# A NaN-skipping row maximum: ten write-backs that go through their elements in another order

## The chip, the cores and the metric

The kernel runs on one core of one Trainium2 chip. The metric is the device time of one execution in microseconds (us). Three engines work on the data: VectorE (DVE in the profile), ScalarE (ACT) and GpSimd (POOL). SyncE (SP) only issues the transfers.

## The reference

```python
def setup_inputs():
    batch, seq, dim = 32, 2048, 2048
    x = np.random.randn(batch, seq, dim).astype(np.float32)
    mask = np.random.rand(batch, seq, dim) < 0.1
    x[mask] = np.nan
    return {"x": x, "axis": -1}

def reference(x, axis):
    return np.nanmax(x, axis=axis).astype(np.float32)
```

The input is 65,536 rows of 2,048 float32 values (537 MB), a tenth of them NaN. The output is the largest value of each row that is no NaN.

## The kernel before, in words

**Cleaning.** [...] Only the upper 16 bits of each float are touched: `xt[:, a:b].bitcast(i16)[:, 1::2]`, a view of int16 elements that lie 4 bytes apart. Two steps do it. ScalarE makes a *key* (line 384 calls the helper whose record is L222): it reads the upper halves of xt and writes a packed uint16 tensor, kt, in which a NaN has become a number of its own. Then the *write-back* turns the key into the upper half again and writes it to xt in place; a NaN comes out as minus infinity. Most write-backs are GpSimd's (line 405, record L232), some are ScalarE's (in `release`, line 357, record L222 again, with `xt<-kt` instead of `kt<-xt`). VectorE then takes the maximum of the cleaned part (line 430, record L239).

**Tiles.** The work is a hand-written list, `TILES`. Sizes are in units of Q = 512 elements per partition, and a full tile is 28 of these (14,336 elements in each of 128 partitions, 7.3 MB). Each entry gives the loads, the pieces that are cleaned, and the pieces of the maximum. A usual tile is `([28], [7, 9, 12], [16, 12])`: one load, three keys with three GpSimd write-backs of 3584, 4608 and 6144 elements, and two reductions. A negative piece is ScalarE's to write back. Entries 8, 16, 24, 32 and 40 of the list (counted from 0) are

```python
([28], [9, 12, -7], [8, 20])
```

There GpSimd writes back 4608 and 6144 elements, ScalarE the last 3584. The first reduction (8) needs only the piece of 9; the second (20) needs the piece of 12 and ScalarE's piece.

**Order of the work.** Three buffers hold tiles (`xts`), three hold keys (`kts`, 6144 elements each). Every engine goes through its instructions in the order of the program and waits on semaphores, which the class `Order` puts down. A load waits for the last reduction of the tile that had its buffer three tiles earlier. A key waits for its load and for the write-backs of what was in its key buffer. In the entries above the order on ScalarE is: key of 9, key of 12, key of 7, write-back of 7, and then the key of 7 of the next tile. The key of 7 in the tile waits for GpSimd's write-back of the piece of 9, since it takes that piece's key buffer.

Of the kernel before, what the change touches and what calls it, by code (L numbers as in the profile page):

```python
# [10 lines left out]
Q = D // 4  # L11
# [51 lines left out]
LEAD = 128  # L63

LANES = 14

# [104 lines left out]
def kernel(  # L173
# [18 lines left out]
    i16, u16 = mybir.dt.int16, mybir.dt.uint16  # L192
# [22 lines left out]
    with tc.tile_critical():  # L215
# [75 lines left out]
        number = 0  # L291
# [6 lines left out]
        for gi, (s, g) in enumerate(zip(rows, GROUPS)):  # L298
            xg = xr[r0 : r0 + P * s].rearrange("(p s) d -> p (s d)", p=P)
            og = of[r0 : r0 + P * s].rearrange("(p s) -> p s", p=P)  # L300
            r0 += P * s
            first = sum(rows[:gi])
            acc = accs[:, first : first + s]
            base = 0
            for loads, pieces, reds in g:
                assert sum(loads) == total(pieces) == sum(reds)
                xt, before = xts[number % BUFS], free[number % BUFS]
                number += 1
                landed = []
                at = 0  # L310
                for c in loads:
                    c *= Q
                    e = order.add(
                        "sp",
                        nc.sync,
                        lambda: nc.sync.dma_start(  # L316
                            out=xt[:, at : at + c], in_=xg[:, base + at : base + at + c]
                        ),
                        before + lanes[turn],
                        lane=f"load{turn}",  # L320
                        step=16,
                    )
                    lanes[turn] = [e]
                    turn = (turn + 1) % LANES
                    landed.append((at, at + c, e))
                    at += c
                clean = []
                after = []
                at = done = 0
                reds = [n * Q for n in reds]  # L330
                part = []
                held = []
                pairs = {}
                if number not in APART:
                    pairs = joints(pieces, [n // Q for n in reds])
                flat = sum((p if isinstance(p, tuple) else (p,) for p in pieces), ())
                half = {}
                piece = 0

                def cleaned(a, b, k, i, e):  # L340

                    nonlocal clock
                    clock += 1
                    both = [(a, b, k, flat[i] < 0, clock)]
                    if i in pairs:
                        if pairs[i] not in half:
                            half[pairs[i]] = both
                            return
                        both += half.pop(pairs[i])
                    for a, b, k, back, when in both:  # L350
                        kfree[k].append((back, when, e))
                        clean.append((a, b, e))

                def name(i):
                    return f"pair{number}_{pairs[i][0]}" if i in pairs else None

                def release():
                    for a, b, k, kp, e, i in held:
                        e = act(
                            [e],  # L360
                            name(i),
                            out=xt[:, a:b].bitcast(i16)[:, 1::2],
                            in_=kp,
                            func=ACT.Copy,
                            bias=float(TOP),
                            scale=-1.0,
                        )
                        cleaned(a, b, k, i, e)
                    held.clear()

                for parts in pieces:
                    parts = parts if isinstance(parts, tuple) else (parts,)
                    c = int(sum(map(abs, parts))) * Q
                    here = [l for a, b, l in landed if a < at + c and b > at]
                    kold = []
                    if used + c > KEYS:
                        key = (key + 1) % NKEYS
                        used = 0
                        kold, kfree[key] = last(kfree[key]), []
                        assert all(k != key for q in half.values() for _, _, k, _, _ in q)  # L380
                        if at + c == sum(loads) * Q:

                            kold = kold + last(kfree[(key + 1) % NKEYS])
                    e_key = act(
                        here + kold,
                        out=kts[key][:, used : used + c],
                        in_=xt[:, at : at + c].bitcast(i16)[:, 1::2],
                        func=ACT.Prelu,
                        bias=EDGE,
                        scale=-1.0,  # L390
                        alpha=float(TOP - LOW) / (EDGE - NAN),
                    )
                    release()
                    for c in parts:
                        back, wait, c = c < 0, isinstance(c, float), int(abs(c)) * Q
                        kp = kts[key][:, used : used + c]
                        used += c
                        to = xt[:, at : at + c].bitcast(i16)[:, 1::2]
                        at += c
                        if back:  # L400
                            held.append((at - c, at, key, kp, e_key, piece))
                            if not wait or at == sum(loads) * Q:
                                release()
                        else:
                            e = pool(
                                [e_key],
                                name(piece),
                                out=to,
                                in0=kp,
                                scalar1=-1.0,  # L410
                                scalar2=float(TOP),
                                op0=ALU.mult,
                                op1=ALU.add,
                            )
                            cleaned(at - c, at, key, piece, e)
                        piece += 1
                        open_ = [h[0] for h in held] + [p[0] for q in half.values() for p in q]
                        while reds and done + reds[0] <= min([at] + open_):
                            n = reds.pop(0)


                            lo = done - 1 if done % D else done
                            done += n
                            row = (base + lo) // D
                            if done % D:
                                m, to = 1, xt[:, done - 1 : done].bitcast(f32)
                            else:
                                m = max(n // D, 1)
                                to = acc[:, row : row + m]
                            e = dve(  # L430
                                [e for a, b, e in clean if b > lo and a < done] + part,
                                nc.vector.tensor_reduce,
                                out=to,
                                in_=xt[:, lo:done]
                                .bitcast(f32)
                                .rearrange("p (c d) -> p c d", c=m),
                                axis=mybir.AxisListType.X,
                                op=ALU.max,
                            )
                            part = [e] if done % D else []  # L440
                            after.append(e)
                free[(number - 1) % BUFS] = after[-1:]
                base += at
            stores.append((og, acc.bitcast(i32)))
            if gi == LATE:
                late_after = after
            elif gi not in FLAGGED:
                continue
            lo, flagged = flagged, first + s
            if gi == LATE:  # L450
                late_acc = accs[:, lo:flagged]
            else:
                e = find(after, accs[:, lo:flagged])
                ready += [e] * (gi + 1 - len(ready))
            if gi == len(GROUPS) - 1:
                ready[LATE] = find_late(late_after, late_acc, late)
# [47 lines left out]
```

## Time and profile before

| | |
|---|---|
| median of 3 runs | 1252.51 us (1252.46 to 1252.6) |
| the profiled execution's own time | 1252.48 us |
| its span in the trace | 1250.7 us |
| busy: POOL / DVE / ACT | 1168.5 (93%) / 1111.4 (89%) / 965.6 (77%) us |
| HBM read | 536.87 MB, 429 GB/s over the span |

The span runs from the first to the last instruction; 1.8 us of the execution lie outside it. Busy time is the time in which an engine executes. A wait is idle time before an instruction, put down to what ended last before it.

### The profile page before, as it was taken

The numbers are of one execution on the slowest core, as the hardware profiler recorded it, in microseconds if no ns is written. First come the engines' busy times: TensorE is split into PE (matmuls) and PEld (weight loads), VectorE is DVE, ScalarE is ACT, GpSimd is POOL, SyncE is SP. The second block draws the span as 40 slices with busy tenths as digits, with TensorE's granted clock in tenths as the row PEclk, the third lists the DMA queues.
The fourth block names the chain that finished last, engine by engine and source line by source line (L and its number), as shares of the span: only waits on it lengthen the run. The fifth ranks groups of instructions, "written<-read, shape, count | busy, mean of one in ns | idle before, by whom it ended". The sixth has DMA issues, their size and how long they took to land.

```text
span 1250.7 us, 891 instructions
## 1 busy us (share of the span) xinstructions
DVE 1111.4 (89%) x179; ACT 965.6 (77%) x273; POOL 1168.5 (93%) x242
## 2 busy tenths in 40 slices
DVE  0888989888889888898988888998888899999999
ACT  3777887778777877788777877777777778999997
POOL 2999989998999899998999899999999999989998
DMA  9999999999999999999999999999999999999997
GB/s 415 440 418 433 440 440 438 413 440 440 440 433 418 440 440 438 429 424 440 440 436 424 431 440 438 436 424 433 440 438 435 422 436 436 425 434 429 431 428 301
DMA packets 15991, 537.20 MB, mean 430 GB/s; under 512 B 2544, under 2 KB 2544, under 8 KB 3568
## 3 DMA queue, kind: packets, MB, share of 16 engines
q1 hardware_dynamic: 15984, 537.14, 99.4%
q14 instruction: 7, 0.06, 0.0%
HBM read 536.87 MB, written 0.26 MB: 429 GB/s over the span
## 4 chain that ended last, share of the span: by engine, by line
DMA 40%; DVE 29%; POOL 22%; ACT 9%; issue 1%; SPq 0%
DMA xt<-in_x_dram 40%; DVE acc L239 29%; POOL xt L232 22%; ACT kt L222 8%; ACT xt L222 1%; SPq L316 0%; DVE acc L245 0%; SPq L499 0%; SPq L215 0%
## 5 line engine op out<-in xcount | busy, mean ns | idle before, releaser
L232 POOL TENSOR_SCALAR xt<-kt 128x3584 int16<-128x3584 uint16 (+11 forms) x236 | 1167.4, 4947 | 77.6 <-ACT kt L222 63.9
L239 DVE TENSOR_REDUCE acc<-xt 128x3 f32<-128x6144 f32 (+4 forms) x175 | 1107.5, 6379 | 135.6 <-POOL xt L232 128.1
L222 ACT ACTIVATE kt<-xt 128x3584 uint16<-128x3584 int16 (+9 forms) x247 | 913.4, 3734 | 278.0 <-DMA xt<-in_x_dram 257.9
L222 ACT ACTIVATE xt<-kt 128x512 int16<-128x512 uint16 (+6 forms) x24 | 52.8, 2202 | 0.7
L245 DVE SCALAR_TENSOR_TENSOR acc<-acc 128x414 f32<-128x414 f32 (+1 forms) x2 | 2.2, 1111 | 0.1
L222 ACT ACT_TABLE_LOAD x1 | 1.3, 1283 | 0.9 <-SPq L215 0.9
L239 DVE TENSOR_REDUCE xt<-xt 128x1 f32<-128x1536 f32 x1 | 1.7, 1743 | 0.0
L278 DVE MEMSET scalars<- 128x1 f32 x1 | 0.1, 59 | 1.0 <-SPq L215 1.0
L260 POOL TENSOR_SCALAR late<-acc 128x91 int32<-128x91 f32 x1 | 0.5, 549 | 0.1
L274 POOL TENSOR_TENSOR acc<-acc,late 128x91 int32<-128x91 int32 x1 | 0.3, 341 | 0.1
L485 POOL MEMSET const-float32-0.0<- 128x1 f32 x1 | 0.1, 98 | 0.2 <-issue 0.2
L222 ACT ACTIVATE scalars<-scalars 128x1 f32<-128x1 f32 x1 | 0.2, 203 | 0.0
L485 POOL MEMSET const-bfloat16-1.0<- 128x1 bf16 x1 | 0.1, 101 | 0.0
L485 POOL MEMSET const-uint8-127<- 128x1 uint8 x1 | 0.1, 101 | 0.0
L485 POOL MEMSET const-float32-1.0<- 128x1 f32 x1 | 0.1, 98 | 0.0
## 6 DMA issues: line engine op xcount, KB each, us to landing
xt<-in_x_dram SPq DMA_DIRECT2D x61, 7168.0 KB, 22.6
xt<-in_x_dram SPq DMA_DIRECT2D x2, 5120.0 KB, 17.4
xt<-in_x_dram SPq DMA_DIRECT2D x3, 2816.0 KB, 22.7
xt<-in_x_dram SPq DMA_DIRECT2D x4, 2048.0 KB, 22.3
xt<-in_x_dram SPq DMA_DIRECT2D x5, 1536.0 KB, 29.1
xt<-in_x_dram SPq DMA_DIRECT2D x2, 3584.0 KB, 24.8
xt<-in_x_dram SPq DMA_DIRECT2D x6, 1024.0 KB, 26.8
xt<-in_x_dram SPq DMA_DIRECT2D x3, 1792.0 KB, 30.1
```

The source lines that it names most:

```text
L222: lambda: nc.scalar.activation(**kw),
L232: lambda: nc.gpsimd.tensor_scalar(**kw),
L239: return order.add("dve", nc.vector, lambda: do(**kw), deps)
L245: lambda: nc.vector.scalar_tensor_tensor(out=acc, in0=acc, scalar=LEAST, in1=acc, op0=ALU.is_ge, op1=ALU.mult,),
L260: lambda: nc.gpsimd.tensor_scalar(out=none, in0=acc, scalar1=LEAST, scalar2=float(0x00400000), op0=ALU.is_lt, op1=ALU.mult,),
L274: lambda: nc.gpsimd.tensor_tensor(out=bits, in0=bits, in1=none, op=ALU.add),
L278: e_warm = order.add("dve", nc.vector, lambda: nc.vector.memset(warm, 1.0), [])
L485: nc = _bacc.Bacc("TRN2", target_bir_lowering=False, num_devices=1)
```

## The change

In entries 8, 16, 24, 32 and 40 of the list, two write-backs each go through their elements in another order: GpSimd's piece of 9 (it begins at 0) and ScalarE's piece of 7 (it ends at the tile's end). GpSimd's piece of 12 stays as it is. Both the input view of kt and the output view of xt are rearranged in the same way, so that each element still goes to its own place. The number and the sizes of the instructions, their waits and every other tile stay.

```diff
+ORDERS = {
+    8: ("p (a b) -> p b a", {"a": 2}),
+    16: ("p (a b) -> p b a", {"b": 512}),
+    24: ("p (a b c) -> p a c b", {"b": 2, "c": 16}),
+    32: ("p (a b c) -> p a c b", {"b": 4, "c": 16}),
+    40: ("p (a b c) -> p a c b", {"b": 8, "c": 4}),
+}
...
+                done_at = total(pieces) * Q
...
+                def inorder(ap, a, b, end):
+                    if number - 1 in ORDERS and (a == 0 or b == end):
+                        how, sizes = ORDERS[number - 1]
+                        return ap.rearrange(how, **sizes)
+                    return ap
...
-                            out=xt[:, a:b].bitcast(i16)[:, 1::2],
-                            in_=kp,
+                            out=inorder(xt[:, a:b].bitcast(i16)[:, 1::2], a, b, done_at),
+                            in_=inorder(kp, a, b, done_at),
...
-                                out=to,
-                                in0=kp,
+                                out=inorder(to, at - c, at, done_at),
+                                in0=inorder(kp, at - c, at, done_at),
```

What the innermost loop of each instruction does now, in bytes from one element to the next (keys are 2 bytes apart in memory's order, the upper halves in xt 4 bytes):

| entry | innermost count | step in kt | step in xt |
|---|---|---|---|
| 8 | 2 | 4608 (GpSimd), 3584 (ScalarE) | 9216, 7168 |
| 16 | 9 (GpSimd), 7 (ScalarE) | 1024 | 2048 |
| 24 | 2 | 32 | 64 |
| 32 | 4 | 32 | 64 |
| 40 | 8 | 8 | 16 |

## The prediction

> **What bounds the kernel now.** I read the page first: busy shares, DMA row, transfers.
>
> ```profile
> DVE 1111.4 (89%) x179; ACT 965.6 (77%) x273; POOL 1168.5 (93%) x242
> ...
> DMA  9999999999999999999999999999999999999997
> ...
> xt<-in_x_dram SPq DMA_DIRECT2D x61, 7168.0 KB, 22.6
> ```
>
> GpSimd is the busiest engine, but the transfers never pause. In the trace the full tiles land every 16.9 us (loads 4 to 57: 16.87 to 17.38). A load takes 22.6 us from issue to landing, so it is issued 5.7 us before the load ahead of it lands. How much of this lead is slack? The first load of all, with nothing before it, brings a seventh of a tile (2.4 us at that pace) and takes 4.7 us; about 2.3 us are fixed. So a load may be issued about 5.7 - 2.3 = **3.4 us** later (the slack S, an estimate) before the DMA engines run dry. Rows bound it: load 60 has a lead of 4.93, load 1 of 4.29, and both still land 16.9 us behind their forerunners, so at least 1.4 us are free; at most 5.7.
>
> Second, the chain of waits around entry 8, in order of time (start, duration, what):
>
> ```profile
> 118.37 22.68 DMA xt<-in_x_dram
> ...
> 141.07 4.05 ACT kt L222
> ...
> 145.19 5.35 POOL xt L232
> ...
> 150.56 3.20 ACT kt L222
> ...
> 153.78 4.20 ACT xt L222
> 157.98 3.17 ACT kt L222
> ...
> 161.22 4.20 POOL xt L232
> ...
> 165.50 5.34 POOL xt L232
> ...
> 170.87 15.16 DVE acc L239 x2
> ...
> 186.04 22.68 DMA xt<-in_x_dram
> ```
>
> Both changed instructions stand in it one behind the other: GpSimd's 4608 at 145.19, ScalarE's 3584 at 153.78, with the key of 7 between them, which waits for the first. Behind them come the next tile's key, its GpSimd work, its reductions and a load. So what the two gain in length is added, and that sum, δ, reaches the load whole.
>
> Third, whether lateness is made good (GpSimd in order of time; in brackets its idle time before):
>
> ```profile
> 145.19 12.46 POOL L232 TENSOR_SCALAR xt<-kt 128x4608 int16<-128x4608 uint16 x2 [1.02 <-ACT kt L222]
> 161.22 16.73 POOL L232 TENSOR_SCALAR xt<-kt 128x3584 int16<-128x3584 uint16 x3 [3.56 <-ACT kt L222]
> 178.13 16.73 POOL L232 TENSOR_SCALAR xt<-kt 128x3584 int16<-128x3584 uint16 x3 [0.17 <-ACT kt L222]
> 195.09 16.73 POOL L232 TENSOR_SCALAR xt<-kt 128x3584 int16<-128x3584 uint16 x3 [0.23 <-ACT kt L222]
> ```
>
> Before a usual tile GpSimd idles some 0.18 us, of which 0.08 stay even without a wait. It recovers 0.10 per tile, 0.7 over the seven tiles between two changed ones, and 1.02 - 0.08 = 0.94 at the next changed one: **1.64 us** per round of eight (R). The 3.56 us recover nothing: there GpSimd waits for ScalarE's path above, which is late itself.
>
> **What the elements cost.** The groups by shape:
>
> ```profile
> L232 POOL TENSOR_SCALAR xt<-kt 128x6144 int16<-128x6144 uint16 x61 | 429.7, 7044 | 6.0 <-ACT kt L222 1.3
> ...
> L222 ACT ACTIVATE kt<-xt 128x6144 uint16<-128x6144 int16 x61 | 324.6, 5321 | 17.2 <-POOL xt L232 17.1
> L232 POOL TENSOR_SCALAR xt<-kt 128x4608 int16<-128x4608 uint16 x53 | 282.8, 5335 | 9.1 <-ACT kt L222 5.4
> ...
> L222 ACT ACTIVATE xt<-kt 128x3584 int16<-128x3584 uint16 x5 | 21.0, 4201 | 0.2
> ...
> L222 ACT ACTIVATE xt<-kt 128x512 int16<-128x512 uint16 x6 | 4.7, 776 | 0.2
> ...
> L232 POOL TENSOR_SCALAR xt<-kt 128x512 int16<-128x512 uint16 x3 | 2.3, 761 | 0.2
> ...
> L222 ACT ACTIVATE kt<-xt 128x512 uint16<-128x512 int16 x1 | 0.6, 613 | 0.0
> ```
>
> Slopes: keys (read at 4-byte steps, written at 2) (5321 - 613)/5632 = 0.836 ns per element. Write-backs (read at 2, written at 4) on GpSimd (7044 - 761)/5632 = 1.116, on ScalarE (4201 - 776)/3072 = 1.115. Two unlike engines pay the same 0.28 ns more when they write at twice the step, so the price is memory's and depends on the step written. That is the only row here that varies with a step.
>
> No row shows a longer step. Bounds, per element: below, 0.836 (the other order even lifts the surcharge); above, 4 × 1.115 = 4.46 (if in memory's order four neighbours share one visit to memory that costs 4.46 ns, and now each pays for its own). Between them I carry the row on: 0.28 for each doubling gives 1.68 ns at 16 bytes, the shortest new step in xt (entry 40). I take **1.68** for all five, double the plain 0.836, as if the price stopped rising there, because 16 bytes is nearest to the row I have; that it stops is a guess.
>
> [...]
>
> **The sum.** Taken away or moved: nothing; ten instructions last longer.
> - GpSimd, each of five: 4608 × (1.68 - 1.116) = 2.60 us.
> - ScalarE, each of five: 3584 × (1.68 - 1.115) = 2.02 us.
> - δ = 4.62 us, on the path whole. What is queued behind: on GpSimd the piece of 12 (with 3.56 us of idle time after it), on ScalarE the next tile's key, and so everything later.
> - Entry 8: δ - S = 4.62 - 3.4 = 1.2 us are lost to a dry DMA queue; lateness stays at 3.4.
> - Entries 16, 24, 32, 40: each finds 3.4 - 1.64 = 1.76 us left, adds 4.62 and loses what is over 3.4: 2.98 each, 11.9 together.
> - After entry 40, 3.4 - 0.7 = 2.7 us of lateness go on through the tiles with pieces of 6, 10 and 12, where GpSimd recovers next to nothing. The tightest lead there (load 60, 4.93) leaves 2.6: 0.1 us lost. Between 1065 and 1145 us GpSimd has eight idle stretches of 7.4 us in total, which take up the rest before the tail, where it never idles.
>
> Total 1.2 + 11.9 + 0.1 = 13.2 us on the profiled execution's 1252.48 (0.03 under the median of 1252.51): **1265.7 us**. S only enters once; with S from 1.4 to 5.7 the sum moves by +2 or -2.3.
>
> **Rivals.**
> 1. *Order costs nothing (ends not slower).* The price of 1.115 may belong to each 2-byte write at a step other than 2, whatever the step; equal slopes on two engines fit that as well. Then 1252.5. The same holds if the other order lifts the surcharge (0.836, δ = -2.3): loads would be issued earlier, but they land every 16.9 us anyway. The point from which it decides: up to δ = 2.0 lateness never reaches 3.4; at δ = 2.5 the loss is about 2.5 us. That is 0.3 ns per element.
> 2. *Heavier.* The surcharge is paid once for four neighbours, 4 × 0.28 = 1.12, now by each: 1.95 ns; or a visit covers two, 2 × 1.115 = 2.23. Then δ = 6.9 or 9.1, and 5δ - S - 4R = 5δ - 10 gives 24 to 36: 1277 to 1288.
> 3. *Much heavier.* 4.46 ns: GpSimd +15.4, ScalarE +12.0, δ = 27.4, loss 127: 1380 us. For it: one price for a partly written stretch explains 1.115 without a second constant. Against it: nothing but that it needs a write unit that takes no second request.
> 4. *Only GpSimd pays*, ScalarE keeping 1.115: δ = 2.6, lateness 2.6, 3.56, then 4.36 three times, loss 0.2 + 3 × 0.96 = 3.0: 1255.5. If only ScalarE pays, δ = 2.0 and nothing is lost. [...]
> 5. *The change does nothing*: views could be merged back into memory's order on the way to the chip. Unlikely, since input and output are given with separate steps: 1252.5.
>
> **How the numbers follow.** A measurement here can tell about 0.2% (2.5 us) from no change. Forecast 0.38 (own range 1260 to 1271); heavier 0.17; much heavier 0.11; only GpSimd, or only some orders, 0.10; nothing 0.24 (a hundredth of it in reserve for faster). Faster needs a transfer pace above that of 61 equal loads: 0.01. Same: 0.23 and a hundredth of the one-engine case, 0.24. Slower 0.75. The range goes from 1252 (nothing) to 1289 (heavier); only the much heavier case and crumbs lie outside, 0.15.
>
> **What would show it.** Right: the five changed GpSimd instructions last some 7.9 us, ScalarE's 6.2; all others stay; the leads shrink from 5.7 to about 2.3 behind entry 8; five landings are late by 1.2 and then 3.0 us, with dips in the DMA row there. Wrong: a changed instruction at 5.3 or 4.2 us (rival 1); durations that differ between the orders (two near elements against nine far ones), which would mean that distance or count matters and not the step being long; or longer instructions without late landings, which would break S or R.

## The result and the profile after

The changed kernel takes **1383.01 us** (1382.03 to 1384.15) against 1252.49 of the kernel before: 1.1042 times as long, 95% interval 1.1023 to 1.1061. That is slower by 130 us, ten times the 13 that the forecast gave, and above its range; it is the *much heavier* rival (1380 us), to which the prediction gave 0.11.

The page of the changed kernel: busy shares, then the DMA rows.

```profile
DVE 1111.9 (81%) x179; ACT 1023.8 (74%) x273; POOL 1246.1 (90%) x242
...
DMA  9999939996699939999399966999999999999997
GB/s 409 445 425 425 452 130 417 429 434 292 266 417 429 434 156 399 422 434 430 123 425 427 440 302 261 420 427 429 442 430 430 441 432 430 431 431 429 431 429 309
```

VectorE works as long as before (1111.9 us against 1111.4). GpSimd works 77.6 us longer, ScalarE 58.2. The transfers, busy for 90% or more of 39 of the 40 slices before, now stop five times (from 340 to 358 us their busy share is 0.00), and afterwards run at the old pace (from the fourth load on, landings 16.9 to 17.3 us apart). The two groups with changed instructions, all instructions of a shape together:

```profile
L241 POOL TENSOR_SCALAR xt<-kt 128x4608 int16<-128x4608 uint16 x53 | 359.6, 6785 | 7.5 <-ACT kt L231 3.8
...
L231 ACT ACTIVATE xt<-kt 128x3584 int16<-128x3584 uint16 x5 | 80.5, 16103 | 0.2
```

ScalarE's five last 16.10 us in the mean instead of 4.20. GpSimd's mean hides five long ones among 53; one by one they last 20.62, 20.84, 20.88, 20.40 and 20.45 us in entries 8, 16, 24, 32 and 40, ScalarE's 16.10, 16.16, 16.27, 15.92 and 16.06. An instruction's share without elements is about 0.19 us (the 761 ns of GpSimd's 512 elements less 512 × 1.116). Less that, the ten cost 4.39 to 4.49 ns per element, with hardly a difference between the orders.

The chain of waits around entry 8 of the changed kernel (start, duration, what):

```profile
145.22 20.63 POOL xt L241
165.87 3.20 ACT kt L231
169.09 16.10 ACT xt L231
...
188.26 4.20 POOL xt L241
```

It is the chain of before with two longer members. What GpSimd does meanwhile, with its idle time ahead of the next tile in brackets:

```profile
145.22 27.78 POOL L241 TENSOR_SCALAR xt<-kt 128x4608 int16<-128x4608 uint16 x2 [1.01 <-ACT kt L231]
188.26 76.89 POOL L241 TENSOR_SCALAR xt<-kt 128x3584 int16<-128x3584 uint16 x14 [15.27 <-ACT kt L231]
```

GpSimd waits 15.27 us for ScalarE where it waited 3.56: the two long instructions stand one behind the other and cover nothing of each other. From 188.26 on it goes through 14 instructions with no more than the usual 0.08 us between them; it is late and catches up slowly.

### The profile page after: what moved, and what is told of

Same layout as the page of the kernel before. It is cut to its first block, busy times and chain, and to the rows that moved or that the text cites. A ratio compares the mean times of both kernels' runs of the same rounds, so it can differ in the third digit from the quotient of the medians.

```text
span 1380.3 us, 891 instructions
## 1 busy us (share of the span) xinstructions
DVE 1111.9 (81%) x179; ACT 1023.8 (74%) x273; POOL 1246.1 (90%) x242
## 4 chain that ended last, share of the span: by engine, by line
POOL 47%; DMA 22%; DVE 17%; ACT 12%; issue 1%; SPq 0%
POOL xt L241 47%; DMA xt<-in_x_dram 22%; DVE acc L248 17%; ACT kt L231 6%; ACT xt L231 6%; SPq L325 0%; DVE acc L254 0%; SPq L515 0%; SPq L224 0%
## 5 line engine op out<-in xcount | busy, mean ns | idle before, releaser
L241 POOL TENSOR_SCALAR xt<-kt 128x3584 int16<-128x3584 uint16 (+11 forms) x236 | 1245.0, 5275 | 129.5 <-ACT kt L231 113.4
L231 ACT ACTIVATE xt<-kt 128x512 int16<-128x512 uint16 (+6 forms) x24 | 112.4, 4682 | 0.7
```

Source lines behind the costliest of these rows:

```text
L231: lambda: nc.scalar.activation(**kw),
L241: lambda: nc.gpsimd.tensor_scalar(**kw),
```

## The experiments

E1, E2 and E5 to E9 were run once each, E3, E4 and E11 four times, E10 ten times.

### Which side pays: input or output

One view of each write-back is rearranged, the other stays, on both engines. First the input alone (E1):

```diff
-    out=inorder(to, at - c, at, done_at),
+    out=to,
```

> Only the input view (kt) is rearranged in the ten write-backs; the output goes in memory's order, so that the cleaned values land in wrong places (left out: the right order of the elements). Theory W (the price is the write's: every visit to a stretch of four neighbours of xt costs 4.46 ns, since each visit writes only a part of it): GpSimd 5.34 us and ScalarE 4.20 us as before, time 1252.5. Theory R (the price is the read's at steps of 8 bytes and more): GpSimd about 20.6, ScalarE 16.1, time 1383. Theory B (a jump costs on either side, the dearer one counts): the same 20.6 and 16.1. If reads cost half of it, 10.4 and 8.1.

Measured 1261.1 us. GpSimd of the input-only kernel in order of time, entry 8 in the first line and entry 16 in the second (each with the piece of 12 behind it, 7.06 and 7.12 us):

```profile
145.53 12.47 POOL L241 TENSOR_SCALAR xt<-kt 128x4608 int16<-128x4608 uint16 x2 [1.02 <-ACT kt L231]
...
281.10 15.40 POOL L241 TENSOR_SCALAR xt<-kt 128x4608 int16<-128x4608 uint16 x2 [1.01 <-ACT kt L231]
```

No theory hit this. In entries 8, 24 and 40 nothing grows (5.34 to 5.41, 4.19 to 4.24 us). In 16 and 32 GpSimd takes 8.21 us and ScalarE 6.4 to 6.5: 1.74 to 1.75 ns per element. So reads have a price of their own, but a small one, and two places in turn are free (entries 8 and 24) while four (entry 32) or nine and seven (entry 16) are not.

Then the output alone (E2):

```diff
-    in0=inorder(kp, at - c, at, done_at),
+    in0=kp,
```

> Only the output view (xt) is rearranged; the keys are read in memory's order (left out: the right order of the elements). Theory W: GpSimd about 20.6 us, ScalarE 16.1 us in all five entries, time 1383. Theory R: 5.34 and 4.20, time 1252.5. Theory B: 20.6 and 16.1.

Measured 1382.5 us, as W said. All five orders cost on both engines, one by one 20.29 to 20.88 us on GpSimd and 15.84 to 16.27 on ScalarE (the group means of the output-only kernel):

```profile
L241 POOL TENSOR_SCALAR xt<-kt 128x4608 int16<-128x4608 uint16 x53 | 359.2, 6778 | 8.1 <-ACT kt L231 4.4
...
L231 ACT ACTIVATE xt<-kt 128x3584 int16<-128x3584 uint16 x5 | 80.2, 16045 | 0.2
```

The write alone makes the whole change: its 1382.5 us lie within the 1382.03 to 1384.15 of both views together, so the reads beside it add nothing that shows.

### Which engine, and what the path makes good

GpSimd alone (E3) and ScalarE alone (E4); the diff of E3, E4 does the same to `in0` and `out` of GpSimd:

```diff
-    out=inorder(xt[:, a:b].bitcast(i16)[:, 1::2], a, b, done_at),
-    in_=inorder(kp, a, b, done_at),
+    out=xt[:, a:b].bitcast(i16)[:, 1::2],
+    in_=kp,
```

> GpSimd's five write-backs are rearranged, ScalarE's go in memory's order. The five last 15.1 to 15.5 us longer, 76.5 in sum. Theory P (the path is serial, with a slack of 1.0 us once, as the landings of the changed kernel suggest, and 1.64 us made good per round): 76.5 - 1.0 - 6.6 = 69 more, 1321.5 us. With the slack of 3.4 of the prediction: 66.5 more, 1319. Theory Q (nothing is made good): 76.5 more, 1329. Theory T (ScalarE's write-back is hidden beside GpSimd's longer one, so that GpSimd alone makes the whole loss): 1383.

> ScalarE's five write-backs are rearranged, GpSimd's go in memory's order. The five last 11.7 to 12.1 us longer, 59.5 in sum, and the key behind each 0.3 longer, 61 in all. Theory P: 61 - 1.0 - 6.6 = 53.4 more, 1306 us; with the slack of 3.4: 51, 1303.5. Theory Q: 1313.5. Theory T: 1252.5.

GpSimd alone: 1323.67 us, ratio 1.057 (1.0554 to 1.0585). ScalarE alone: 1306.39 us, ratio 1.0432 (1.0415 to 1.045). The two excesses, 71.2 and 53.9 us, add up to 125, and both changes together make 130: the path is serial. Theory T is out on both sides, and Q (nothing is made good) missed by 5.3 and 7.1 us. P came within 2.2 and 0.4 us. The hit on ScalarE alone is luck in part: P took 7.6 us as made good, more than there were, and counted 1.5 us for the longer keys behind the write-backs. Those keys begin 0.5 us before the write-back ends and end 2.98 us after it (3.16 before the change), so they add nothing to the path.

From the spans, what each kernel made good is its instructions' growth less the growth of its span: 136.0 - 129.6 = 6.4 us in the changed kernel, 76.5 - 70.8 = 5.7 with GpSimd alone, 59.6 - 53.5 = 6.1 with ScalarE alone. That is about 1.2 us for each of the five entries in all three.

### What a write costs: steps and runs

From here on `ORDERS` names the order for each entry and engine, on both views. Steps (E5):

```diff
+    8: {"pool": ("p (a b) -> p b a", {"b": 2}), "act": ("p (a b) -> p b a", {"b": 2})},
+    16: {"pool": ("p (a b) -> p b a", {"b": 4}), "act": ("p (a b) -> p b a", {"b": 4})},
+    24: {"pool": ("p (a b) -> p b a", {"b": 3}), "act": ("p (a b) -> p b a", {"b": 7})},
...
```

> The ten write-backs go through memory upwards, but in longer steps (several passes): entry 8 with 8 bytes in xt, 16 with 16, 24 with 12 (GpSimd) and 28 (ScalarE), 32 with 32; entry 40 goes through each stretch of four neighbours in the order 0, 2, 1, 3. Theory W (each visit to a 16-byte stretch that is only partly written costs 4.46 ns, however many of its elements come in that visit): per element 2.23 in entry 8 (GpSimd 10.5 us, ScalarE 8.2), 4.46 in 16 (20.6, 16.1), 3.34 and 4.46 in 24 (15.6, 16.1), 4.46 in 32, 1.115 in 40 (5.34, 4.20); time about 1333. Theory D (my prediction's: 0.28 ns more for each doubling of the step): 1.40 in 8 (6.6, 5.2), 1.68 in 16 (7.9, 6.2), 1.56 and 1.9 in 24. Theory J (any departure from memory's order costs 4.46): all ten 20.6 and 16.1.

Measured 1331.26 us. GpSimd of the kernel with steps; the first line holds entry 8 and the piece of 12 behind it, the last line entry 16 alone:

```profile
145.34 17.59 POOL L241 TENSOR_SCALAR xt<-kt 128x4608 int16<-128x4608 uint16 x2 [1.02 <-ACT kt L231]
...
288.47 20.66 POOL L241 TENSOR_SCALAR xt<-kt 128x4608 int16<-128x4608 uint16 x1 [0.60 <-ACT kt L231]
```

Runs (E6):

```diff
+    8: {"pool": ("p (a b c) -> p b a c", {"a": 2, "c": 2}), "act": ("p (a b c) -> p b a c", {"a": 2, "c": 2})},
...
+    24: {"pool": ("p (a b c) -> p b a c", {"a": 2, "c": 3}), "act": ("p (a b c) -> p b a c", {"a": 2, "c": 7})},
...
```

> The ten write-backs alternate between the two halves of their piece, with runs of neighbours of a given length: entry 8 runs of 2, 16 of 4, 24 of 3 (GpSimd) and 7 (ScalarE), 32 of 6 and 14, 40 of 8 and 1. Theory W, by counting visits to 16-byte stretches per element: 2.23 ns in entry 8 (10.5, 8.2 us); 1.115 in 16 (5.34, 4.20); in 24 half a visit per element, 2.23 (10.5), and 2.5 visits in 7, 1.59 (5.9); in 32 one visit in 3, 1.49 (7.1), and 4 in 14, 1.27 (4.8); in 40 1.115 (5.34) and 4.46 (16.1). Time about 1279. Theory U (the unit is 8 bytes, a visit costing 2.23, and a jump adds the rest): runs of 4 and 8 would be dearer than 1.115. Theory J: all 20.6 and 16.1.

Measured 1277.34 us. ScalarE's key of 7 and, in the second line, its write-back in entry 8 of the kernel with runs (runs of 2; 8.2 us expected):

```profile
155.52 3.19 ACT L231 ACTIVATE kt<-xt 128x3584 uint16<-128x3584 int16 x1 [5.13 <-POOL xt L241]
158.75 7.99 ACT L231 ACTIVATE xt<-kt 128x3584 int16<-128x3584 uint16 x1
```

A visit is here a series of accesses, one right behind the other, to the same 16-byte stretch of xt. Both kernels together, against visits at 4.46 ns each (ns per element, an instruction's duration less 0.19 us, divided by its elements):

| order of the writes to xt | visits per element | by the count | measured |
|---|---|---|---|
| step 8 bytes | 1/2 | 2.23 | 2.23, 2.22 |
| step 12 (GpSimd) | 3/4 | 3.34 | 3.34 |
| step 16 | 1 | 4.46 | 4.44, 4.45 |
| step 28 (ScalarE), 32 | 1 | 4.46 | 4.31; 4.27, 4.25 |
| 0, 2, 1, 3 inside a stretch | 1/4 | 1.115 | 1.12, 1.12 |
| runs of 2 | 1/2 | 2.23 | 2.18, 2.18 |
| runs of 3 (GpSimd) | 1/2 | 2.23 | 2.27 |
| runs of 4 | 1/4 | 1.115 | 1.11, 1.11 |
| runs of 6 (GpSimd) | 1/3 | 1.49 | 1.48 |
| runs of 7 (ScalarE) | 5/14 | 1.59 | 1.60 |
| runs of 14 (ScalarE) | 2/7 | 1.27 | 1.26 |
| runs of 8 (GpSimd) | 1/4 | 1.115 | 1.11 |
| runs of 1 (ScalarE) | 1 | 4.46 | 4.44 |

One number explains all of it to within 5%, on both engines. Theories D, J and U are out. The price is neither the step's nor the jump's; it is that of a visit, 4.46 ns, and memory's own order is the case of a quarter of a visit per element. That the stretch is 16 bytes shows in the table, above all in its runs of 3, 6, 7 and 14, which straddle the ends of stretches (2.27, 1.48, 1.60 and 1.26 ns measured, 2.23, 1.49, 1.59 and 1.27 by the count). Stretches of 8 bytes at 2.23 ns would give 1.49 for the runs of 3 (measured 2.27), stretches of 32 bytes at 8.92 ns would give 8.92 for steps of 32 (measured 4.25 to 4.27).

### Why a visit costs that much: halves of words

Whole words, in memory's order and in runs (E7; the edit on GpSimd's output, ScalarE's is edited likewise):

```diff
-    out=inorder(to, at - c, at, done_at),
+    out=inorder(xt[:, at - c : at].bitcast(f32) if number - 1 in ORDERS and at - c == 0 else to, at - c == 0 and "pool"),
```

> In the five entries the ten write-backs write whole float32 words (4 bytes, both halves) instead of the upper halves; the values there are those of the key as a float (left out: the cleaned values of these pieces). Entry 8 in memory's order, 16 in runs of 1 word alternating between the halves of the piece, 24 of 2, 32 of 4 (16 bytes), 40 of 3 (GpSimd) and 7 (ScalarE). Theory W (a stretch that is filled in its visit has no surcharge, a partly written one costs 4.46): entry 8 0.836 ns (4.04, 3.18 us, shorter than before), 16 4.46 (20.6, 16.1), 24 2.23 (10.5, 8.2), 32 0.836 (4.04, 3.18), 40 2.23 (10.5) and 1.43 (5.3). Theory V (every visit costs 4.46, filled or not): 8 and 32 1.115 (5.34, 4.20), 40 2.23 and 1.59 (5.9).

Measured 1257.46 us. GpSimd in the kernel that writes words, first entry 8 (in memory's order), then entry 16 (one word per visit, 8.32 us, with the piece of 12 behind it), and the means of the five on each engine:

```profile
145.23 4.03 POOL L241 TENSOR_SCALAR xt<-kt 128x4608 f32<-128x4608 uint16 x1 [1.05 <-ACT kt L231]
...
281.09 15.48 POOL L241 TENSOR_SCALAR xt<-kt 128x4608 f32<-128x4608 uint16 x2 [1.02 <-ACT kt L231]
```

```profile
L241 POOL TENSOR_SCALAR xt<-kt 128x4608 f32<-128x4608 uint16 x5 | 25.7, 5140 | 5.1 <-ACT kt L231 5.1
...
L231 ACT ACTIVATE xt<-kt 128x3584 f32<-128x3584 uint16 x5 | 19.8, 3963 | 0.2
```

Entries 8 and 32 are as W said: 4.03 and 3.19 us, 0.83 ns per word, which also ends V. But W failed in entry 16: one word per visit costs 1.76 ns (8.32 and 6.49 us), not 4.46, and two words per visit 0.91 or 0.92 each, not 2.23. In entry 40 the runs of 3 words cost 1.03 ns per word (4.95 us, not 10.5) and the runs of 7 0.92 (3.47 us, not 5.3). A partly filled stretch is not the reason.

The same question on the packed side (E8):

```diff
-    out=kts[key][:, used : used + c],
-    in_=xt[:, at : at + c].bitcast(i16)[:, 1::2],
+    out=inorder(kts[key][:, used : used + c], "key" if at == 0 else at + c == done_at and "key7"),
+    in_=inorder(xt[:, at : at + c].bitcast(i16)[:, 1::2], "key" if at == 0 else at + c == done_at and "key7"),
```

> All write-backs in memory's order; instead ScalarE's keys of 9 and of 7 in the five entries alternate between the two halves of their piece, on both sides: they write the packed kt (8 elements in 16 bytes). Key of 9 (4.04 us before): runs of 1, 2, 4, 8, 12 in entries 8 to 40; key of 7 (3.19): 7, 16, as before, 1, 4. Theory W: 20.7, 10.5, 5.3, 4.04, 4.5 us; 4.4, 3.19, 3.19, 16.1, 4.2. Theory X (the price belongs to the odd halves of xt alone, packed writes are free of it): all 4.04 and 3.19. Time by W about 1287.

Measured 1280.5 us. The key of 9 in entry 8 and the key of 12 behind it are the first line of the keys kernel's ScalarE, in entry 16 the last:

```profile
141.26 25.68 ACT L231 ACTIVATE kt<-xt 128x4608 uint16<-128x4608 int16 x2 [4.07 <-DMA xt<-in_x_dram]
...
292.40 9.53 ACT L231 ACTIVATE kt<-xt 128x4608 uint16<-128x4608 int16 x2 [3.59 <-DMA xt<-in_x_dram]
```

The lone 2-byte element costs the full price in the packed kt too (20.57 us; 16.10 for the key of 7), which ends X. The price is not that of the keys' own rearranged reads: with two places in turn these come to 1.06 ns per element at most (E9 below). W missed the rest: pairs 4.33 us instead of 10.5, runs of 4, 8 and 12 all 4.04, runs of 7 3.85 instead of 4.4. Two neighbours in kt fill a 4-byte word; two neighbours in xt are halves of two words, and they cost 2.18 ns each in the table above against 0.90 here. So theory H: **a visit that leaves a 4-byte word half written costs 4.46 ns, a visit that writes whole words 1.76**, and no visit less than the plain 0.836 ns for each of its elements. The runs of 7 in kt, which split words at their ends, come to 1.05 ns by H and measured 1.02; the runs of 2, 3 and 7 words of E7 come to 0.88, 1.00 and 0.91 and measured 0.91 or 0.92, 1.03 and 0.92. The small differences may be the reads', which were rearranged alike. H was made from these figures, so they are no test of it; E11, expected before it ran, tests its case of one word per visit.

The change's own five orders in whole words (E11); the same edit on GpSimd's output:

```diff
-    out=inorder(xt[:, a:b].bitcast(i16)[:, 1::2], a, b, done_at),
+    out=inorder(xt[:, a:b].bitcast(f32) if number - 1 in ORDERS and b == done_at else xt[:, a:b].bitcast(i16)[:, 1::2], a, b, done_at),
```

> The change as it is, with its five orders on both engines, but the ten write-backs write whole float32 words to xt instead of the upper halves (left out: the cleaned values of these pieces). Theory H (a visit that leaves a 4-byte word half written costs 4.46 ns, one of whole words 1.76): one word per visit in all five orders, so about 1.76 per element, GpSimd 8.3 us, ScalarE 6.5; 5.2 us longer together, loss 5 x 5.2 - 1.0 - 6.6 = 18, 1271 us. Theory W (any partly filled 16-byte stretch costs 4.46): 20.6, 16.1, 1383; the two orders of words tried so far spoke against it, three are new. Theory G (one order of the five is dearer in words, as two of five were for reads alone): entries 16 and 32 longer than 8, 24 and 40.

Measured 1273.4 us, ratio 1.0168 (1.0151 to 1.0185). All five orders cost the same again to 5% (GpSimd 8.08 to 8.51 us, ScalarE 6.31 to 6.61):

```profile
L241 POOL TENSOR_SCALAR xt<-kt 128x4608 f32<-128x4608 uint16 x5 | 41.6, 8324 | 3.2 <-ACT kt L231 3.2
L231 ACT ACTIVATE xt<-kt 128x3584 f32<-128x3584 uint16 x5 | 32.5, 6499 | 0.2
```

H holds, W and G are out. In entries 16 and 32 the reads alone cost as much (E1: 8.21 us on GpSimd, 6.4 to 6.5 on ScalarE); in 8, 24 and 40, where they are free beside a write-back (E1: 5.34 to 5.41 and 4.19 to 4.24 us), the price is the write's. The ten instructions grow by 26.4 us, the span by 20.2: again 6.2 made good, where the 1271 us expected had counted on 7.6.

### Reads by themselves

Inputs alone, in other orders, on the write-backs and on the key of 12 (E9):

```diff
-    in_=xt[:, at : at + c].bitcast(i16)[:, 1::2],
+    in_=inorder(xt[:, at : at + c].bitcast(i16)[:, 1::2], "key" if at == 9 * Q else None),
```

> Only inputs are rearranged (left out: the right order of the elements); outputs go in memory's order, so that a read shows where it exceeds 1.115 ns (write-backs) or 0.836 (key of 12, 5.32 us before). GpSimd's input goes round 3, 4, then upwards in steps of 16 bytes, of 8 bytes, round 6 far places (entries 8 to 40); ScalarE's round 4, 7, upwards in 16, in 8, round 4 with 2 neighbours each; the key of 12 reads xt round 2, 3, 4, 4 with 2 neighbours each, upwards in 16 bytes. Theory O (two stretches are held open for reads, and with three or more each read of another stretch costs 1.74): GpSimd 8.2, 8.2, 8.2, 5.34, 8.2 us; ScalarE 6.4, 6.4, 6.4, 4.2, 4.2; keys 5.32, 10.9, 10.9, 5.5, 10.9. Theory F (it takes four or more): 3 places are free: 5.34 for GpSimd in entry 8, 5.32 for the key in 16. Theory E (a visit costs 1.74 whatever is held, but alternation between two is merged): upwards in 16 bytes as O.

Measured 1271.26 us. ScalarE's write-back in entry 8 of the reads kernel, with four places in turn (4.20 us before):

```profile
155.06 6.45 ACT L231 ACTIVATE xt<-kt 128x3584 int16<-128x3584 uint16 x1
```

Neither O nor F holds throughout. On write-backs F is right: three places in turn are free on GpSimd (5.38 us), four, six and seven cost 1.74 to 1.79 ns, steps of 16 bytes 1.81 to 1.84; steps of 8 bytes (5.42 us) and four places with two neighbours each (4.22 on ScalarE) are free. The keys have a lower floor (0.84 ns) and show a little more: 1.06 with two places, 1.16 with three, 1.78 with four, 0.91 with two neighbours at each of four. Why two and three places lie between is not settled.

### Another order that costs nothing

Runs of four neighbours in all five entries (E10):

```diff
+    8: {"pool": ("p (a b c) -> p b a c", {"a": 2, "c": 4}), "act": ("p (a b c) -> p b a c", {"a": 2, "c": 4})},
...
```

> All five entries rearranged, both engines, both sides: the write-backs alternate between the two halves of their piece in runs of four neighbours, as far apart as in entry 8 of the changed kernel (9216 and 7168 bytes). Theory W: every visit still covers one whole stretch of four, so all ten instructions last 5.34 and 4.20 us and the time is 1252.5. Theory J (any other order costs): 20.6 and 16.1, 1383. Theory N (the number of jumps counts: a quarter as many as in the changed kernel): 9.2 and 7.2 us, 1278.

Measured 1252.71 us, ratio 1.0 (0.999 to 1.0009). All five entries jump as far as entry 8 of the change does, between two places, in whole stretches:

```profile
L241 POOL TENSOR_SCALAR xt<-kt 128x4608 int16<-128x4608 uint16 x53 | 282.6, 5333 | 9.1 <-ACT kt L231 5.4
...
L231 ACT ACTIVATE xt<-kt 128x3584 int16<-128x3584 uint16 x5 | 20.9, 4177 | 0.2
```

J and N are out: between two places, neither order nor jumps cost anything as long as a visit takes all that it has to write in its stretch. Jumps among more places were not tried in this form.

## Why the prediction was wrong, point by point

- **The path was right.** Both instructions add up, the sum reaches the load, GpSimd's 3.56 us of idle time help nothing, the rest of the program is unchanged, and the landings fall behind in five places (gaps of 40.5 to 41.7 us instead of 16.9). E3 and E4 show it. One reason given ahead of the prediction is not right: the key of 7 takes the buffer of the tile before's piece of 12, not that of the piece of 9. It waits for the piece of 9 because the program lets a tile's last key also wait for the buffer that the next key will take (`kold = kold + last(kfree[(key + 1) % NKEYS])`). That wait puts the two long instructions one behind the other; no run tried the kernel without it.
- **The price per element was wrong, and with it everything.** The step that failed is *I take 1.68, as if the price stopped rising there, because 16 bytes is nearest to the row I have*. It measured 4.39 to 4.49 ns. The row that I carried on (0.28 ns more when the step doubles) was no row of steps at all. It compared packed writes, which fill whole words, with half-word writes four to a visit; 0.28 was the difference of two regimes. The number that decides, 4 × 1.115 = 4.46, stood in the text as the upper bound, and its mechanism as a rival, right to 3 us; only its *partly written stretch* had to become a half-written word (E7, E8). The seven rows of shapes could not tell the two readings apart. Going by the nearest row decided between them, and wrongly.
- **1.68 is near the price of whole words and of reads, by luck.** E11 gave 1.71 to 1.81 with the change's own orders, E1 1.74 for reads; the row from which 1.68 was carried on has to do with neither. In E1 the reads of two places in turn were free beside a write-back (GpSimd 5.34 and 5.36 us in entries 8 and 24, whose steps in kt are 4608 and 32 bytes); entries 16 and 32 took 8.21 us, entry 32 with the step of entry 24, so the step alone does not give the price. ScalarE pays the same per element in entries 16 and 32 (6.4 to 6.5 us against 4.20).
- **The slack was too large.** S was put at 3.4 us; about 1.2 was there, less than the 1.4 that the rows were said to show. In the changed kernel load 11, the first behind the change, is issued 27.2 us later than before and lands 24.4 later, so it finds 2.8 us of slack: alone in the queue it takes 20.1 us from issue to landing, 3.2 more than the 16.9 of its bytes, where the first small load had shown 2.3. Another 1.5 us go two loads later. Load 13 is issued 3.2 us before its forerunner lands and still comes 18.4 us after it, though load 12 lost nothing with a lead of 3.1. It is the same in all five rounds, and with leads of 4.4 to 4.8 the next loads come after 16.9 to 17.3 us. Why a load within the stream needs more lead stays open. R was then wrong in use: with 1.2 us of slack no more than 1.2 can be made good per round, not 1.64, and S does not enter only once where it is below R. With the measured growth and the 1.2 us of E3 and E4 the sum is 136.0 - 5 × 1.2 = 130 for 129.6 measured. S and R were 4 us off, the price 113 (5 × (27.2 - 4.62)).
- **The other cases.** *Order costs nothing* is true only where a visit takes its whole stretch (E10, and entry 40 of E5). *Only GpSimd pays* is false; both pay alike (4.39 to 4.49 ns per element on each in the changed kernel). Views were not merged back. The lateness left after entry 40 was made good before the tail, as written: from load 61 on (counted from 0) the leads are those of before to 0.1 us.

No run beats the kernel before. In E7 eight of the ten write-backs got cheaper, and the two dearer ones of entry 16 made it 5 us slower; that cheaper ones alone bring nothing, because loads land 16.9 us apart whatever GpSimd does, was argued and not tried by itself.

## What to carry to other kernels

Count visits, not steps: for an output of ScalarE or GpSimd (VectorE's were not tried), ask how many separate visits to 16-byte stretches an instruction makes, and whether each visit writes whole 4-byte words (1.76 ns a visit here, 4.46 where a word was left half written). Keep the elements of one stretch together in the order, above all where 2-byte elements are written 4 bytes apart. Jumps between two places were then free (E10: 5.33 and 4.18 us, as before); with four places or more in turn look at the reads too, which cost up to 1.84 ns each (E9). And when a row admits two readings whose outcomes differ by ten times, the unlucky reading that needs only one constant deserves more than a tenth.

## What the runs showed of the hardware that was not expected

- Half-word writes cost 4.46 ns per visit (E5 and E6, to within 5%), whole-word writes 1.76 (E7; 1.71 to 1.81 in E11) or 0.83 per element, if that is more (E7, entries 8 and 32), on ScalarE and GpSimd alike; in the changed kernel far and near, two places or nine make 2.4% of difference (20.40 to 20.88 us). Why half words cost more stays open.
- A usual write-back pays this price too: four half words per visit, 1.115 ns instead of the 0.83 that the same elements cost as whole words in E7.
- Two places in turn, near or far, are free for the reads of a write-back, four are not (5.34 and 5.36 against 8.21 us).
- The third load behind each of the five stops, issued 2.7 to 3.2 us before its forerunner landed, came 1.5 to 1.8 us late, though the second lost nothing with the same lead and a load alone needs only 3.2 us beyond the 16.9 of its bytes.
